# One block around the whole program, ordered by the scheduler's timing simulation (hybrid backbone, gated delta scan in chunks of 64)

## The chip, the core and the metric

The kernel runs on one core of a Trainium2 chip. The core has five engines, each with its own queue that it works through in order: TensorE (PE) for matmuls, VectorE (DVE), ScalarE (ACT), GpSimd (POOL), and SyncE (SP), which issues nearly all DMAs here. They meet through semaphores: an instruction waits at the head of its queue until what it needs is done, and everything behind it waits too. The metric is the device time of one execution in microseconds (us), lower is better; the numbers are medians over runs.

## What is computed

One inference step of a hybrid backbone with two layers, on 128 context tokens and 1024 latent tokens (nine tiles of 128 tokens in all), width 1024, in float32. The core of the reference:

```
def trunk_layer(x, cvec, lp, ctx):
    sh1, sc1, g1, sh2, sc2, g2 = jnp.split(jax.nn.silu(cvec) @ lp['w_ada'] + lp['b_ada'], 6, axis=-1)
    h = rmsnorm(x, lp['g_pre_mix']) * (1.0 + sc1) + sh1
    m, extras = mixing(h, lp, ctx)
    x = x + g1 * rmsnorm(m, lp['g_post_mix'])
    h = rmsnorm(x, lp['g_pre_ffn']) * (1.0 + sc2) + sh2
    f = conv_ffn(h, lp['w_up'], lp['ffn_conv_w'], lp['ffn_conv_b'], lp['w_down'])
    x = x + g2 * rmsnorm(f, lp['g_post_ffn'])
    return x, extras
```

`mixing` projects `h` once and splits the result among three groups: a conformer convolution (width 31, layer norm, swish); a gated delta net with four heads, scanned forwards and backwards in chunks of 64, whose step is

```
        v_new = ui - jnp.einsum('bhcd,bhde->bhce', wi, state)
        o = jnp.einsum('bhcd,bhde->bhce', qd, state) + jnp.einsum('bhij,bhje->bhie', it, v_new)
        state = state * gl[..., None, None] + jnp.einsum('bhcd,bhce->bhde', kd, v_new)
```

and neighbourhood attention with four heads. A second projection joins the three. The modulation (`w_ada`) is a vector product of its own.

## The kernel before, in words

The class `K` builds the program (L1639 and on, `run`), once for the whole network. Every large matmul is made in three passes with split operands: high by high, low by high, high by low (`mm3`, L429 to L431; the z gates and the attention's projections have the same three on L618). Such a group of 24 matmuls has 128x386 outputs and is called dense work here.

A layer runs in this order in the code:

- Start (layer 0 only): `ada_pe` loads the modulation weights (`rawa`, L315) and multiplies them (L317, L323); token tiles `x` come in on L406; `tail_weights` loads `rawt` (L494); each token tile is turned on PE (L387) and goes through the tail of the input projection.
- Heads 0 and 1 of the delta net: dense work (`gdn_dense`), decays, then `preps`, which inverts the chunk matrices: `fd` and `F` to and from memory (L677, L1619, L1629), `DA` loaded in eight pieces (L820), blocks multiplied on PE (L841, L854).
- `gdn_scan` of heads 0 and 1: 18 chunk steps forwards and backwards for each head. One step is L921 (state times keys and queries), `t` on DVE, L929, `ys` and `y` on ACT, L943 (state update) and L946, then two updates of `S` and an addition into `o` on DVE.
- While that scan runs, dense work of heads 2 and 3 (`gdn_piece`), of the convolution (`conf_dense`), its depthwise taps (`conf_conv`, the DVE operation named `cu`, in eight pieces of 31 taps, lowered in priority by `LOW`), and the inverse of heads 2 and 3 (operation `e` on DVE, L1626, L1627).
- Then the z gates, `gdn_out` of heads 0 and 1 (L993), the late part of heads 2 and 3 (`gdn_late`: loads `kq` L757, `DI` and `DA` L760, `ktm` L763, products L771, blocks), the attention's projections, and in layer 0 a part of the next modulation (`ada_fill`, L271 and L273).
- The scan of heads 2 and 3 with the attention woven into it. Its loads are `V` (L1217), `oq` from the cached keys (L1225), `qk` (L1233) and the bias `whib` and `RB` (L1168, in pieces); L1250 turns the cached keys.
- The convolution's output (`conf_out`, L1071 and L1102), more `ada_fill`, the output projection, and the feed-forward part with its own depthwise convolution.

What sets the order: the scheduler places the instructions of one block by its cost estimate and its priorities, and each engine's queue follows that placement. Three sections are exempt for PE, where the code says `manual_schedule(engines=ENG)` with `ENG = {PE}`: the start with the tail projection, the scan of heads 2 and 3 with the attention, and the end of a layer with the next one's tail. There PE's order is as written. SP, DVE, ACT and POOL have no section of that kind. The program was one block before and is one after.

Of the kernel before, what the change touches and what calls it, by code (L numbers as in the profile page):

```python
# [1783 lines left out]


def emit(tc, I, O):
    with ExitStack() as ctx:
        K(ctx, tc, I, O).run()


# [57 lines left out]
```

## Time and profile before

| | before |
|---|---|
| median of 3 runs | 3492.34 us |
| lowest, highest | 3491.82, 3495.67 us |
| the profiled execution, its own time | 3500.02 us |
| its span in the profile | 3498.2 us |
| mean granted clock of TensorE | 0.959 |
| PE busy | 3251.0 us (93%) |
| DVE busy | 2127.5 us (61%) |
| ACT, POOL busy | 1293.4 us (37%), 1026.5 us (29%) |

The profile shows each instruction with its start and duration; the span is first to last. The granted clock is 1 where TensorE has its 2.4 GHz and 0.5 where it has 1.2 GHz; a mean between them says what part of a stretch was at which. Stretches of one stage are compared by a table: length, then busy time of each engine with the instructions' number, then the clock. A wait is named after the instruction that waited and the one whose result came last.

### The profile page before, as it was taken

To read this page: it belongs to the slowest core of one execution; us is meant where nothing else is said; L and a number is where in the kernel's file an instruction comes from. 1 tells how busy PE (TensorE), PEld (TensorE's weight loads), DVE (VectorE), ACT (ScalarE), POOL (GpSimd) and SP (SyncE) were. 2 spreads that over 40 slices of the span, in tenths; PEclk is the share of its full clock that TensorE was granted. 3 is DMA by queue.
4 is the path that set the end of the run, shared out by engine and by line. 5 is a ranking of instruction groups with operands and counts; after the bars stand their busy time and mean duration, and the time that the engine had idled before them with its cause. 6 is when DMAs were issued, how large, how long until landed. Compare 5 with 4: busy or idle time off the path is not lost. (4 is left out here: it accounts for less than half of the span.)

```text
span 3498.2 us, 52694 instructions
## 1 busy us (share of the span) xinstructions
PE 3251.0 (93%) x19868; PEld 2842.8 (81%) x19868; DVE 2127.5 (61%) x4128; ACT 1293.4 (37%) x2887; POOL 1026.5 (29%) x933
## 2 busy tenths in 40 slices
PE   8999996978999999999989989879599999999997
PEld 5997775626899988989989977877388999999997
DVE  4677776744556666655476767878654444444446
ACT  4333333534433333333254423346443222222223
POOL 3421213123544334434234311221343112211114
PEclk9999998988999999999999999989699999999999
DMA  5332454255323222222134223642452111111113
GB/s 194 103 81 82 144 157 92 56 184 152 117 85 94 73 76 88 82 64 78 41 134 126 64 70 92 188 99 62 128 167 71 37 37 44 54 43 43 37 37 132
DMA packets 288339, 324.08 MB, mean 93 GB/s; under 512 B 152143, under 2 KB 213855, under 8 KB 286998
## 3 DMA queue, kind: packets, MB, share of 16 engines
q1 hardware_dynamic: 288086, 320.72, 30.8%
q8 instruction: 157, 2.57, 0.3%
q14 instruction: 96, 0.79, 0.1%
HBM read 250.68 MB, written 69.95 MB: 92 GB/s over the span
## 5 line engine op out<-in xcount | busy, mean ns | idle before, releaser
L431 PE MATMUL d<-hhi,wlo 128*128 128x386 f32 (+1 forms) x3072 | 1056.0, 344 | 5.5 <-POOL wlo L420 5.5
L429 PE MATMUL d<-hhi,whi 128*128 128x386 f32 (+1 forms) x3072 | 1056.3, 344 | 3.5 <-DVE cv L124 3.4
L430 PE MATMUL d<-hlo,whi 128*128 128x386 f32 (+1 forms) x3072 | 1055.4, 344 | 3.2 <-issue 3.2
L420 POOL TENSOR_TENSOR wlo<-raw,whi 128x1024 fp32r<-128x1024 f32 x136 | 343.6, 2527 | 1151.7 <-ACT whi L121 1082.9
L124 DVE SCALAR_TENSOR_TENSOR cv<-d,fvec,cv 128x384 f32<-128x384 f32 (+1 forms) x528 | 325.3, 617 | 459.5 <-ACT cv L121 451.0
L431 PEld LDWEIGHTS d<-hhi,wlo 128*128 128x128 f32 x3072 | 584.5, 190 | 18.5 <-issue 10.0
L429 PEld LDWEIGHTS d<-hhi,whi 128*128 128x128 f32 x3072 | 585.8, 191 | 14.6 <-issue 12.3
L430 PEld LDWEIGHTS d<-hlo,whi 128*128 128x128 f32 x3072 | 585.4, 191 | 7.4 <-issue 5.7
L1541 DVE TENSOR_TENSOR f<-d,f 128x512 f32<-128x512 f32 x360 | 245.2, 687 | 163.6 <-PE d L431 161.6
L121 ACT ACTIVATE cv<-d,fvec 128x384 f32<-128x384 f32 (+1 forms) x264 | 174.6, 663 | 440.9 <-PE d L431 432.4
L429 PE MATMUL d<-wdh,ahi 128*128 128x512 f32 x792 | 316.1, 399 | 11.0 <-DVE f L1541 9.1
L430 PE MATMUL d<-wdl,ahi 128*128 128x512 f32 x792 | 313.6, 396 | 0.0
L431 PE MATMUL d<-wdh,alo 128*128 128x512 f32 x792 | 312.7, 395 | 0.0
L124 DVE SCALAR_TENSOR_TENSOR cu<-cu,vec 128x292 f32<-128x292 f32 (+1 forms) x480 | 253.6, 554 | 4.0
L121 ACT ACTIVATE whi<-raw 128x1024 fp32r<-128x1024 f32 x136 | 143.6, 1056 | 161.4 <-PE d L430 132.1
L429 PEld LDWEIGHTS d<-wdh,ahi 128*128 128x128 f32 x792 | 149.1, 188 | 50.5 <-DVE f L1541 14.4
L223 POOL TENSOR_TENSOR adacc<-adacc,adpr 128x512 f32<-128x512 f32 x112 | 153.2, 1368 | 124.8 <-ACT adpr L121 97.1
L431 PEld LDWEIGHTS d<-wdh,alo 128*128 128x128 f32 x792 | 148.9, 188 | 36.1 <-issue 0.7
L430 PEld LDWEIGHTS d<-wdl,ahi 128*128 128x128 f32 x792 | 148.9, 188 | 34.3 <-issue 1.4
L121 ACT ACTIVATE adpr<-adraw,cs 128x512 f32<-128x512 f32 x112 | 80.9, 723 | 241.7 <-POOL adacc L223 193.0
L1528 POOL TENSOR_TENSOR wdl<-rawd,wdh 128x512 fp32r<-128x512 f32 x88 | 115.4, 1312 | 182.9 <-ACT wdh L121 182.9
L1517 DVE TENSOR_TENSOR alo<-sg,ahi 128x384 fp32r<-128x384 f32 x132 | 111.3, 843 | 70.8 <-ACT ahi L121 70.5
(349 smaller groups left out, 5222.4 us busy)
## 6 DMA issues: line engine op xcount, KB each, us to landing
raw<-in_w_up_t SPq DMA_DIRECT2D x88, 512.0 KB
adraw<-in_w_ada SPq DMA_DIRECT2D x112, 256.0 KB
raw<-in_w_in_t SPq DMA_DIRECT2D x48, 512.0 KB
rawd<-in_w_down SPq DMA_DIRECT2D x88, 256.0 KB
xs<-x SPq DMA_DIRECT2D x27, 512.0 KB
x<-xs SPq DMA_DIRECT2D x27, 512.0 KB
rawa<-in_w_ada SPq DMA_DIRECT2D x24, 512.0 KB
x<-in_x SPq DMA_DIRECT2D x18, 512.0 KB
```

The source lines that it names most:

```text
L121: return self.nc.scalar.activation(out=out, in_=in_, func=func, **kw)
L124: return self.nc.vector.scalar_tensor_tensor(out=out, in0=in0, scalar=s, in1=in1, op0=op0, op1=op1, **kw)
L223: nc.gpsimd.tensor_tensor(out=acc[:, 1, :], in0=acc[:, 1, :], in1=pr, op=ALU.add)
L420: nc.gpsimd.tensor_tensor(out=lo[:, :n], in0=raw[:, :n], in1=hi[:, :n].bitcast(F32), op=ALU.subtract)
L429: nc.tensor.matmul(out, shi, mhi, start=(i == 0), stop=False)
L430: nc.tensor.matmul(out, shi, mlo, start=False, stop=False)
L431: nc.tensor.matmul(out, slo, mhi, start=False, stop=(i == n - 1))
L1517: nc.vector.tensor_tensor(out=lo[:, :n], in0=sg[:, :n], in1=hi[:, :n].bitcast(F32), op=ALU.subtract)
L1528: nc.gpsimd.tensor_tensor(out=lo, in0=raw[:, :512], in1=hi[:].bitcast(F32), op=ALU.subtract)
L1541: nc.vector.tensor_tensor(out=f[t][:, cs], in0=ps, in1=f[t][:, cs], op=ALU.add)
```

## The change

`emit` puts the whole program into a block with `schedule_with_timeline_sim=True`, so that the scheduler takes its other, more detailed timing model for placing instructions. The instructions are the same on every engine (PE 19,868 with its waits left out, DVE 4,128); only their order, and with it the waits, differs.

```
 def emit(tc, I, O):
-    with ExitStack() as ctx:
-        K(ctx, tc, I, O).run()
+
+    with tc.block(schedule_with_timeline_sim=True):
+        with ExitStack() as ctx:
+            K(ctx, tc, I, O).run()
```

Line numbers above this place stay; the three manual sections keep PE's order. The first place that matters is the queue of SP at the start. Before:

```order
L315 DMA rawa<-in_w_ada 128x1024 x14
L494 DMA rawt<-in_w_tail 128x544
L315 DMA rawa<-in_w_ada 128x1024 x2
L494 DMA rawt<-in_w_tail 128x544 x2
L406 DMA x<-in_x 128x1024 x2
L494 DMA rawt<-in_w_tail 128x544
L406 DMA x<-in_x 128x1024 x5
L416 DMA raw<-in_w_in_t 128x1024 x2
L406 DMA x<-in_x 128x1024 x2
```

After, at the same place in the queue:

```order
L315 DMA rawa<-in_w_ada 128x1024 x6
L494 DMA rawt<-in_w_tail 128x544 x2
L406 DMA x<-in_x 128x1024 x4
L315 DMA rawa<-in_w_ada 128x1024 x4
L494 DMA rawt<-in_w_tail 128x544 x2
L315 DMA rawa<-in_w_ada 128x1024 x2
L406 DMA x<-in_x 128x1024 x3
L315 DMA rawa<-in_w_ada 128x1024 x2
L416 DMA raw<-in_w_in_t 128x1024 x2
L315 DMA rawa<-in_w_ada 128x1024 x2
L406 DMA x<-in_x 128x1024 x2
```

The modulation weights are spread among the token tiles, and their last two loads stand behind seven of these.

The second place is the scan of heads 0 and 1 in layer 0. DVE's queue in its middle, before (`t`, `S` and `o` are the scan's own; `cu` is the depthwise convolution, `cv` and `cp` the projections' short convolution):

```order
L124 SCALAR_TENSOR_TENSOR t<-a,ne,V 128x128
L124 SCALAR_TENSOR_TENSOR cu<-cu,vec 128x292 x2
L124 SCALAR_TENSOR_TENSOR t<-a,ne,V 128x128
L124 SCALAR_TENSOR_TENSOR cu<-cu,vec 128x292
L124 SCALAR_TENSOR_TENSOR S<-S,ex,b 128x128
L124 SCALAR_TENSOR_TENSOR S<-S,ex,c 128x128
```

After, also in the middle (`e` is the inversion of heads 2 and 3):

```order
L124 SCALAR_TENSOR_TENSOR S<-S,ex,b 128x128
L124 SCALAR_TENSOR_TENSOR S<-S,ex,c 128x128
L1626 TENSOR_TENSOR e<-e 72x368
L124 SCALAR_TENSOR_TENSOR cu<-cu,vec 128x291
L959 TENSOR_TENSOR o<-a,o 128x128
L124 SCALAR_TENSOR_TENSOR t<-a,ne,V 128x128
L124 SCALAR_TENSOR_TENSOR cu<-cu,vec 128x292
L1627 TENSOR_TENSOR e<-e 72x2x23x8
L124 SCALAR_TENSOR_TENSOR cu<-cu,vec 128x291
L124 SCALAR_TENSOR_TENSOR cu<-cu,vec 128x292
L1626 TENSOR_TENSOR e<-e 72x396
```

All eight pieces of `cu` and the whole inversion of heads 2 and 3 now stand inside this scan. PE's queue in the same scan's last steps, before:

```order
L929 MATMUL a<-V,XN 64x128 x2
L431 MATMUL d<-hhi,wlo 128x386
L921 MATMUL a<-S,kq 64x128 x3
L943 MATMUL b<-ys,ktm 128x128
L943 MATMUL c<-ys,ktm 128x128
L946 MATMUL a<-y,DI 64x128 x2
L921 MATMUL a<-S,kq 64x128
L429 MATMUL d<-hhi,whi 128x388
```

After:

```order
L929 MATMUL a<-V,XN 64x128 x2
L929 MATMUL a<-t,XN 64x128 x2
L943 MATMUL b<-ys,ktm 128x128
L943 MATMUL c<-ys,ktm 128x128
L946 MATMUL a<-y,DI 64x128 x4
L929 MATMUL a<-V,XN 64x128 x2
L921 MATMUL a<-S,kq 64x128 x4
```

No dense matmul is left between the last steps; all of it, the z gates' and the attention's projections too, stands ahead of them.

The third place is PE's queue behind the attention of layer 0, where the modulation fill (`b<-rawa,cs`) meets the convolution's output. Before:

```order
L273 MATMUL b<-rawa,cs 2x512 x8
L278 MATMUL b<-rawa,ones 2x512
L291 MATMUL b<-ident,rawa 128x2 x4
L1071 MATMUL a<-ident,cl 128x128 x4
L1102 MATMUL c<-ident,xh 128x128
L1071 MATMUL a<-ident,cl 128x128 x2
```

After:

```order
L993 MATMUL c<-ident,on 128x128 x18
L273 MATMUL b<-rawa,cs 2x512 x7
L1071 MATMUL a<-ident,cl 128x128 x2
L273 MATMUL b<-rawa,cs 2x512
L278 MATMUL b<-rawa,ones 2x512
L1071 MATMUL a<-ident,cl 128x128 x2
```

The convolution's transposes begin behind the first of four fill chunks, where before they followed the fourth; the output projection's matmuls follow among the later chunks. Besides this, SP's queue now has the attention's loads (`V`, `oq`, `qk`) ahead of the late heads' `kq`, `DI`, `ktm` and `DA`, where before it had them behind.

## Rows read from the trace of the kernel before

**Rows 1.** The page: busy time and share of each engine; the convolution's taps.

```profile
PE 3251.0 (93%) x19868; PEld 2842.8 (81%) x19868; DVE 2127.5 (61%) x4128; ACT 1293.4 (37%) x2887; POOL 1026.5 (29%) x933
...
L124 DVE SCALAR_TENSOR_TENSOR cu<-cu,vec 128x292 f32<-128x292 f32 (+1 forms) x480 | 253.6, 554 | 4.0
```

**Rows 2.** Stretches: length, busy us PE, PEld, DVE, ACT, POOL (count), clock, DMA share, GB/s.

```profile
0.00:86.10 86.10, 70.88 (x368) 51.68 (x369) 37.09 (x114) 39.17 (x73) 25.55 (x50) 0.96 0.58 197
...
278.10:391.90 113.80, 112.52 (x972) 77.67 (x971) 82.94 (x249) 46.92 (x165) 13.15 (x18) 1.00 0.22 66
391.90:567.50 175.60, 156.93 (x1120) 136.68 (x1118) 131.11 (x268) 56.02 (x161) 41.99 (x31) 0.94 0.53 156
567.50:741.40 173.90, 133.37 (x1222) 93.40 (x1222) 125.25 (x361) 87.27 (x277) 31.77 (x56) 0.85 0.35 74
741.40:784.10 42.70, 36.02 (x85) 6.29 (x83) 6.36 (x12) 10.66 (x20) 13.07 (x8) 0.90 0.85 284
784.10:813.50 29.40, 20.70 (x74) 14.35 (x74) 13.85 (x37) 10.96 (x22) 10.50 (x20) 0.65 0.34 100
...
935.00:1800.00 865.00, 854.36 (x4448) 791.14 (x4447) 522.61 (x738) 307.31 (x484) 336.17 (x234) 1.00 0.26 79
...
2060.00:2175.00 115.00, 110.82 (x946) 76.43 (x945) 80.68 (x242) 44.81 (x158) 10.33 (x7) 0.99 0.22 65
2175.00:2326.00 151.00, 140.72 (x1091) 133.13 (x1088) 125.71 (x257) 59.01 (x167) 38.48 (x40) 0.95 0.55 158
2326.00:2486.00 160.00, 129.61 (x1235) 94.00 (x1233) 130.39 (x372) 87.62 (x278) 32.15 (x56) 0.89 0.33 69
2486.00:2528.00 42.00, 14.68 (x41) 7.12 (x42) 23.20 (x52) 18.04 (x37) 21.42 (x27) 0.50 0.55 171
...
2650.00:3498.00 848.00, 828.85 (x4310) 774.68 (x4309) 414.83 (x612) 234.33 (x370) 187.15 (x114) 0.99 0.15 52
```

**Rows 3.** Waits of PE: waiter, cause, us in all, times, longest; whole span.

```profile
PE P L1250 <- DMA oq<-in_cache: 23.5, 2, 11.8
...
PE a L929 <- DVE t L124: 10.5, 7, 5.7
PE a L841 <- DVE XN L832: 10.4, 2, 5.6
...
PE a L921 <- DVE o L959: 6.1, 1, 6.1
```

**Rows 4.** The first 90 us: GB/s in 40 slices; the ada matmuls; PE's timeline (start, us).

```profile
GB/s 47 95 54 324 377 413 393 297 300 317 282 280 325 282 351 346 363 364 262 237 240 304 317 226 212 1 58 0 68 1 58 0 3 55 58 7 58 174 20 143
...
L317 PE MATMUL d<-rawa,cb x64: 592/592/1190, 9.1 to 39.2; 128*128 128x512 f32 x64
...
46.91 0.59 PE L429 MATMUL d<-thi,hhi 128*128 128x272 f32 x1 [0.47 <-ACT hhi L121]
```

**Rows 5.** Timeline of the first step of the scan of heads 0, 1.

```profile
278.13 0.66 PE L921 MATMUL a<-S,kq 128*64 128x128 f32 x8
...
281.51 0.34 DVE L124 SCALAR_TENSOR_TENSOR S<-S,ex,c 128x128 f32<-128x128 f32 x1
```

**Rows 6.** Stretches of `cu` alone (DVE, clock); one of all engines as in 2.

```profile
660.00:742.00 82.00, 31.41 (x62) 0.80 0.24 65
2420.00:2490.00 70.00, 28.86 (x56) 0.86 0.22 55
...
580.00:600.00 20.00, 6.92 (x54) 5.16 (x52) 4.32 (x14) 3.64 (x10) 1.52 (x4) 0.66 0.76 106
```

**Rows 7.** Issues of the `DA` pieces (ns min/median/max, first to last start); layer 1's next scan.

```profile
L820 SPq DMA_DIRECT2D DA<-fy x32: 326/496/2552, 253.1 to 2277.1; - x32
...
2329.39 0.66 PE L921 MATMUL a<-S,kq 128*64 128x128 f32 x8
```

## The prediction

> **What bounds the kernel now.** I read the page's busy times first. TensorE (PE) is busy 93% of the span and VectorE (DVE) 61% [rows 1], so a new order can win only what PE loses: its idle time and its time at the lower clock level. Then I read a table of stretches [rows 2]; the reader is to compare PE's busy time with the stretch's length, and the granted clock with 1. Both feed-forward stages (865 and 848 us) keep PE busy 854 and 829 us at a clock of 0.99 or more: nothing to win in half of the span. The losses lie in the mixing stages: start (70.9 of 86.1), scan of heads 2 and 3 with the attention (133.4 of 173.9 at 0.85 in layer 0, 129.6 of 160 at 0.89 in layer 1), the modulation fill and the convolution's output in layer 0 (56.7 of 72.1), the latter in layer 1 (14.7 of 42 at 0.50). Third, the waits of PE [rows 3]: the largest is L1250, which waits twice some 11.8 us for the DMA that brings the cached keys `oq`.
>
> **What the change moves.** No instruction is added or removed. The sum is made on the profiled execution (3500.0 us, 3498.2 of them span) and carried to the median, which is 7.7 us lower, by difference.
>
> *Feed-forward.* Both orders agree here but for a place or so: 0.
>
> *Start: loss.* SP issues its loads in turn. Before, all 16 `rawa` loads stand ahead of the token tiles, with one `rawt` among them; after, the last two stand behind 7 token tiles of 512 KB, 3 more `rawt` of 272 KB and 2 `raw` of 512 KB, 5.4 MB. The slices of the DMA row show about 330 GB/s while the loads run [rows 4], so these land 16 us later. The last ada matmul starts at 39.2, the first tail matmul at 46.9 [rows 4]. The modulation vector gates every token's turn, so about 16 us pass through, less some 5 us since the tokens then are already there and the first transposes done (the 7.7 us from 39.2 to 46.9 shrink). +11, bounds 0 (PE was itself the slower: 64 matmuls took from 9.1 to 39.2) and +16.
>
> *Preparation of heads 0 and 1: gain.* L841 waits 4.8 and 5.6 us, once per layer [rows 3]. After, some 15 us more of dense matmuls stand ahead of it. That dense work is only brought forward, so just the wait goes: -8 for both layers, bounds -10 and 0.
>
> *Scan of heads 0 and 1 and the late preparation of heads 2 and 3.* Here is the heart of it. Before, PE's scan instructions have 2 to 8 dense matmuls between them, and the rest of the dense work covers the late chain. In layer 0 the stretch from scan to scan is 113.8 + 175.6 = 289.4 us with 112.5 + 156.9 = 269.4 us of PE work; in layer 1 115 + 151 = 266 with 251.5 [rows 2]. After, 14 to 30 dense matmuls stand between a step's instructions until the dense work is used up. Adding the trace's durations of what now stands from the first to the last scan instruction: PE 240 us, of the 269.4 in layer 0; 15 went ahead of the scan and 14 stand behind it. DVE gets the convolution's `cu` (218 in place of 40, at some 0.5 us in a row [rows 1]) and the inversion's `e`: 83.0 becomes 216 us. So PE stays the longer engine, but with less margin. I reckon 10 us of idle for that. The last 11 of 36 steps have under 4 us of PE work each: two heads run in alternation, and a step alone takes from 278.13 to 281.85, 3.7 us [rows 5]. Six such pairs need 25 us; PE's work of 19 us is inside. Filled part 222 + 10 + 25 = 257. Then the late chain, bare: loads, blocks, inverse, with 14 us of PE work. For heads 0 and 1 it took from the first `DA` load at 253.1 to the first scan matmul at 278.1, 25 us [rows 5, 7], beside dense work; the steps ahead of that (`kq` products, `DA` and `DI`) and the output transposes add about 10. I take 35; bounds 20 and 60. Layer 0: 15 + 257 + 35 = 307 against 289.4: +18. Layer 1, by the same way: 13 + 241 + 35 = 289 against 269 up to its next scan: +20. Bounds for each -10 and +45. What covers the late chain today is the dense work of the z gates and attention projections; that cover is what the change spends.
>
> A rule of the Trainium skill speaks against this move: "Perfetto Trace Analysis", section "Optimization Strategy", says that where the contended engine changes over time, interleaving those regimes can help. Before, a chain-bound regime and a PE-bound one are interleaved for the late heads, and the trace agrees in so far as PE is busy 157 of 175.6 us there; after, they are apart. How much that costs is the first rival below.
>
> *Attention with the scan of heads 2 and 3: gain.* PE's order is written by hand in this section and stays. SP issues the loads of the attention (`V`, `oq`, `qk`) after the change ahead of the late heads' own `kq` loads, where before they follow them and the late chain. So the 11.7 us at L1250 should go, in each layer. DVE no longer has the convolution here: 31.4 us of `cu` in 660 to 742, 28.9 in layer 1 from 2420 on [rows 6], and the L929 and L921 waits of 5.7 and 6.1 us [rows 3] are waits for DVE results queued behind it. -23.5 in layer 0. With fewer holes PE should be less at the lower level: 580 to 600 runs at 0.66 with 6.9 us busy [rows 6]; I add -6. -29, bounds -50 (idle 40.5 and some clock) and -10. Layer 1 has only the 11.8 and some 4 us of L929: -18, bounds -35 and -5.
>
> *Convolution output, modulation fill, output projection: gain.* In layer 0 PE did four chunks of fill, then the convolution's transposes, then the projection. After, transposes begin behind the first chunk, and projection triples fill between chunks. Idle there is 72.1 - 56.7 = 15.4 us, and the clock is 0.90 and 0.65 [rows 2], which by the stretch lengths is 4 + 10 us of clock. Idle and half of the rest, less what the fill's own loads still hold back (DMA share 0.85): -17, bounds -30 and 0. In layer 1 only a few triples move ahead of the last transposes: -4, bounds -15 and +5.
>
> **Sum.** 11 - 8 + 18 + 20 - 29 - 18 - 17 - 4 = -27. 3492.3 - 27 = 3465.
>
> **Rivals.**
> - *Slower: the bare late chain.* Its place is between the last scan step of heads 0, 1 and the first of heads 2, 3. For: in layer 1 it took 52 us from its last `DA` load at 2277.1 to the scan at 2329.4 [rows 7], and nothing fills it now. Against: the chain then shared PE and DVE with other work. At 60 us per layer in place of 35, with the loads waiting for buffers that the scan frees last, the sum is -27 + 50 = +23: 3515. It decides from 35 + 13.5 = 48 us per layer on.
> - *Slower: the waits of the attention stay.* Earlier in SP's queue helps only where the buffer is free and the data are there. If both waits and the holes remain, 29 + 18 come back: +20, 3512. Against: `oq` is filled from an input, in a queue that had late loads ahead of it.
> - *The order changes little.* PE is in order and 93% busy; gains in the attention and costs in the scan could cancel within 7 us: 3492.
> - *More gain.* The late chain begins in the last scan steps, since its `kq` products stand among them in PE's new order. Then the +18 and +20 fall to about 0: -65, 3427.
>
> **How the numbers follow.** Forecast (-8 to -55) 0.46, more gain 0.12, little change 0.13, bare chain 0.19, waits stay 0.10. Hence faster by over 0.2% (about what a measurement of this kernel can tell from no change, 7 us) 0.58, within 0.13, slower 0.29. The range for 8 in 10 runs from 3425 (more gain) to 3525 (bare chain, with a late start); as forecasts of both signs hold much of the chance, the likeliest one's own range is 3437 to 3484.
>
> **What would show it.** Right: the wait of L1250 is gone from PE's waits; no `cu` during the attention; attention stretches of some 145 us; the first tail matmul near 58 us; a hole of some 20 to 25 us of PE idle between the two scans. The scan of heads 0 and 1 should last about 257 us in layer 0 with PE busy over 0.9 of it until its last steps. Wrong: a late stretch over 48 us, DVE the engine that PE waits for all along the scan (then 216 us of DVE work was not the smaller load), or L1250 still waiting.

## The result and the profile after

The new order is slower: 3537.43 us median (3532.86 to 3538.2) against 3493.8 us for the kernel before on the same chip, a ratio of 1.0122 with a 95% interval of [1.0105, 1.014]. The forecast was 3465, faster; the range of 3425 to 3525 does not hold the time either. The profiled execution has a span of 3535.6 us, 37.4 more than before, at a mean granted clock of 0.947 in place of 0.959.

The page of the new order, its busy times and the taps:

```profile
PE 3268.9 (92%) x19868; PEld 2857.9 (81%) x19868; DVE 2159.0 (61%) x4128; ACT 1295.5 (37%) x2887; POOL 1037.3 (29%) x933
...
L124 DVE SCALAR_TENSOR_TENSOR cu<-cu,vec 128x292 f32<-128x292 f32 (+1 forms) x480 | 252.8, 557 | 0.9
```

Against [rows 1] the instructions are the same in number, and the taps cost the same. PE is busy 17.9 us more with the same matmuls: they ran longer, at the lower clock level.

The table of stretches of the new order (length, then busy us of PE, PEld, DVE, ACT, POOL with counts, clock, DMA share, GB/s). In layer 0: start; scan of heads 0 and 1; from scan to scan; attention; convolution output and fill; projection; FFN. In layer 1: from scan to scan; attention; convolution output; projection:

```profile
0.00:90.10 90.10, 71.46 (x369) 51.51 (x370) 39.74 (x114) 39.04 (x73) 25.89 (x50) 0.96 0.50 190
294.30:549.90 255.60, 242.13 (x1627) 192.65 (x1627) 217.12 (x527) 75.91 (x215) 46.40 (x49) 0.97 0.41 119
549.90:606.20 56.30, 29.95 (x398) 21.43 (x397) 24.98 (x48) 30.64 (x113) 17.41 (x22) 0.50 0.58 147
606.20:755.00 148.80, 128.55 (x1216) 92.37 (x1216) 90.27 (x280) 83.19 (x272) 16.54 (x32) 0.89 0.21 52
755.00:825.70 70.70, 64.50 (x192) 23.59 (x192) 21.93 (x48) 20.27 (x40) 23.09 (x28) 0.86 0.67 222
825.70:956.20 130.50, 111.88 (x532) 94.83 (x532) 60.84 (x100) 56.79 (x121) 57.01 (x72) 0.95 0.44 140
956.20:1791.90 835.70, 825.45 (x4312) 768.08 (x4313) 511.16 (x712) 297.61 (x466) 328.06 (x219) 0.99 0.25 76
2314.10:2367.40 53.30, 28.87 (x395) 20.63 (x396) 24.82 (x47) 31.49 (x115) 16.18 (x19) 0.53 0.62 163
2367.40:2514.20 146.80, 128.21 (x1217) 92.41 (x1218) 90.25 (x279) 83.18 (x272) 16.48 (x32) 0.90 0.21 48
2514.20:2561.60 47.40, 29.27 (x104) 20.37 (x103) 21.47 (x45) 18.33 (x36) 23.17 (x28) 0.63 0.47 156
2561.60:2693.00 131.40, 113.15 (x534) 95.40 (x532) 62.64 (x99) 56.98 (x119) 56.02 (x71) 0.94 0.43 139
```

Read it beside [rows 2]. The scan has swallowed the dense work (255.6 us, PE busy 0.95 of it), and what follows it is naked, that is, the late chain runs there with no dense work beside it: 56.3 us with 29.95 of PE work at a clock of 0.50, and 53.3 us in layer 1. The attention is the gain, 148.8 in place of 173.9 us.

PE's longest waits in the new order (us in all, times, longest):

```profile
PE c L993 <- DVE zt L124: 38.2, 14, 8.6
PE d L429 <- DVE cv L124: 25.8, 4, 8.1
PE d L429 <- ACT chi L121: 16.5, 3, 8.3
...
PE a L929 <- DVE t L124: 9.7, 10, 3.2
```

The same three first waits in the kernel before:

```profile
PE c L993 <- DVE zt L124: 19.4, 7, 4.8
...
PE d L429 <- ACT chi L121: 5.5, 3, 4.2
...
PE d L429 <- DVE cv L124: 5.1, 5, 1.8
```

L1250, the largest of [rows 3], is gone as forecast, and the longest at L929 is 3.2 in place of 5.7 us. What grew in their place is L993 (the output of the heads; 22.9 of its 38.2 us lie in the two naked stretches), L429 for `chi` (the projection), and L429 for `cv`, of which 16.0 us are the FFN's first taps of the two layers.

The account by stages, from the two traces with the same marks (end of the start, first instruction of each scan, last transposed output of the attention, first tap of the FFN; the FFN of layer 0 ends with its last `cv` on ACT). The last column is what the term was off by:

| stage | forecast | measured | off |
|---|---|---|---|
| start | +11 | 90.0 - 86.1 = +3.9 | -7 |
| to the scan of heads 2, 3, layer 0 | -4 + 18 = +14 | 516.3 - 481.5 = +34.8 | +21 |
| attention, layer 0 | -29 | 148.8 - 173.9 = -25.1 | +4 |
| convolution output, projection, layer 0 | -17 | 201.2 - 198.0 = +3.2 | +20 |
| FFN, layer 0 | 0 | 835.8 - 839.2 = -3.4 | -3 |
| to the scan of heads 2, 3, layer 1 | -4 + 20 = +16 | 575.5 - 550.8 = +24.7 | +9 |
| attention, layer 1 | -18 | 146.8 - 160.8 = -14.0 | +4 |
| convolution output, projection, layer 1 | -4 | 178.8 - 164.7 = +14.1 | +18 |
| FFN and end | 0 | 842.5 - 843.4 = -0.9 | -1 |
| sum | -27 | +37.3 | +64 |

Two groups of terms make nearly all of it: the way to the second scan (+29) and the stretch from the attention to the FFN (+38). The experiments go to these two, and to the attention, where the forecast came out but its reasons had not been taken apart. One caution holds for all of them: an edit gives the scheduler a new program, and other places move by a few us too. In the four kernels below whose edit leaves the stretch from the attention to the FFN alone (the bias pieces, the other buffer, the two with cover), it took 195.8 to 201.6 us in layer 0 and 177.2 to 180.1 in layer 1. So a stage's length is compared first, the total second, and a few us in a stage are little.

### The profile page after: what moved, and what is told of

Read it like the earlier page. It is cut to its first block, busy times and chain, and to the rows that moved or that the text cites. A ratio compares the mean times of both kernels' runs of the same rounds, so it can differ in the third digit from the quotient of the medians.

```text
span 3535.6 us, 52748 instructions
## 1 busy us (share of the span) xinstructions
PE 3268.9 (92%) x19868; PEld 2857.9 (81%) x19868; DVE 2159.0 (61%) x4128; ACT 1295.5 (37%) x2887; POOL 1037.3 (29%) x933
## 5 line engine op out<-in xcount | busy, mean ns | idle before, releaser
L429 PE MATMUL d<-hhi,whi 128*128 128x386 f32 (+1 forms) x3072 | 1052.9, 343 | 26.7 <-DVE cv L124 25.8
L429 PEld LDWEIGHTS d<-hhi,whi 128*128 128x128 f32 x3072 | 584.0, 190 | 36.0 <-ACT cv L121 16.6
L429 PE MATMUL d<-wdh,ahi 128*128 128x512 f32 x792 | 317.3, 401 | 8.4 <-DVE f L1541 8.4
L429 PEld LDWEIGHTS d<-wdh,ahi 128*128 128x128 f32 x792 | 149.4, 189 | 46.8 <-DVE f L1541 12.7
L1528 POOL TENSOR_TENSOR wdl<-rawd,wdh 128x512 fp32r<-128x512 f32 x88 | 116.1, 1319 | 171.3 <-ACT wdh L121 171.2
```

The lines of the kernel that those rows point to most:

```text
L429: nc.tensor.matmul(out, shi, mhi, start=(i == 0), stop=False)
L1528: nc.gpsimd.tensor_tensor(out=lo, in0=raw[:, :512], in1=hi[:].bitcast(F32), op=ALU.subtract)
```

## Experiments on the naked late chain

**Bias pieces in SP's queue.** In the new order, loads of the attention's bias (`whib`, `RB`) stand on SP among the late heads' loads. This kernel puts the bias pieces (L1168) behind the last `DA` load, which it keeps in `lastDA` (what stands under `issue_after(x)` comes behind x in its queue):

```
+            with self.tc.issue_after(self.lastDA):
                 nc.sync.dma_start(out=RB[...], in_=I["rpb"][...])
```

> The new order, with one edit: the 64 small loads of the attention's bias (RB, whib) of a layer are issued by SP behind the last DA load of the late heads, not between the loads of the late chain. Theory (SP's queue sets the length of the late chain, some 85 issues in 41 us at 0.48 us each, about half of them bias): the stretch between the two scans falls from 56 and 53 us to about 42 each, and part is given back where the attention waits for its bias; in all 3505 to 3525 us. Rival (the chain of blocks, inverse and copies sets it, whoever issues): both stretches stay above 50 us and the time within 6 us of 3537.

Measured: 3531.32 us, ratio 1.0118 [1.0094, 1.0141]; the naked stretches 52.8 and 55.5 us where they were 56.3 and 53.3. The pieces were not what held it.

**Another buffer for `DA`.** `gdn_late` puts `DA` into the buffer with the tag `o`, in which the output of the first scan's head lies until `gdn_out` has read it. SP's queue in the new order, from 555.86 us (start, us, instruction):

```profile
555.86 4.12 SPq L1168 DMA_DIRECT2D whib<-in_rpb  x7
560.08 0.94 SPq L1004 DMA_DIRECT2D cat<-zt  x2
561.07 0.78 SPq L1168 DMA_DIRECT2D whib<-in_rpb  x2
561.94 0.35 SPq L760 DMA_DIRECT2D DA<-dec  x1
```

The first `DA` load of the late heads goes out at 561.94, 12 us after the scan's end at 549.9, and the loads of the blocks (L820) only from 566.46 on. This kernel lets `DA` and the scan's `V` change places:

```
-        DA = hpool.tile([...], F32, tag="o", name="DA", bufs=1)
+        DA = hpool.tile([...], F32, tag="V", name="DA", bufs=1)
-        V = hpool.tile([...], F32, tag="V", name="V", bufs=1)
+        V = hpool.tile([...], F32, tag=vtag, name="V", bufs=1)
```

(`vtag` is "o" for the late heads, and their output takes "V".)

> The new order, with the late heads' DA tile put into the place of the values V of heads 0 and 1, which the scan frees, in place of the tile of their outputs o, which gdn_out frees last; the late V takes the place of o. Theory (in the bare late chain DA waits for gdn_out of the same place, at 562 and 576 us in the profile, so the two chains run one behind the other): the stretch between the scans falls from 56 and 53 us to 40 to 45 each, the time to 3505 to 3518 us. Rival (the chain is as long without that wait): both stretches above 50 us, time within 6 us of 3537.

SP's queue after the edit, from the scan's end at 550.0:

```profile
550.26 0.42 SPq L760 DMA_DIRECT2D DI<-dec  x1
550.73 0.36 SPq L1168 DMA_DIRECT2D RB<-in_rpb  x1
551.14 5.78 SPq L820 DMA_DIRECT2D DA<-fy  x4
```

The stretch of layer 0 in that kernel, columns as above:

```profile
550.00:595.60 45.60, 26.74 (x396) 20.88 (x395) 19.31 (x43) 24.68 (x98) 11.10 (x18) 0.54 0.61 158
```

Measured: 3523.61 us, 1.0088 [1.0063, 1.0112], 14 us under the new order's median, though the two intervals still touch; the naked stretches 45.6 and 45.1 us. `DA`'s blocks now load 15 us earlier, and 8 to 11 us of each naked stretch were this buffer. First scan and chain together took 301.3 us in layer 0 and 281.4 in layer 1; the new order and the four kernels that leave both alone (stores, order of the code, low parts, FFN's vector) lie at 311.9 to 316.6 and 290.3 to 299.6. The remaining 45 us are still 10 above the 35 forecast.

**Why 45 and not 35.** The same instructions stand in the trace before, beside dense work. The groups of PE in its stretch from 391.9 to 567.5 (busy us, mean ns, idle before):

```profile
L993 PE MATMUL c<-ident,on 128*128 128x128 f32 x18 | 4.5, 288 | 4.6 <-DVE zt L124 3.4 <-ACT on L121 1.2
L841 PE MATMUL a<-XN,DA 32*32 32x32 f32 x144 | 3.6, 192 | 0.0
...
L655 PE MATMUL a<-ident,kq 128*128 128x128 f32 x18 | 2.8, 282 | 0.0
```

and in the naked stretch of the new order, 549.9 to 606.2:

```profile
L993 PE MATMUL c<-ident,on 128*128 128x128 f32 x18 | 7.0, 454 | 12.4 <-DVE zt L124 11.9 <-ACT on L121 0.6
L841 PE MATMUL a<-XN,DA 32*32 32x32 f32 x144 | 6.1, 238 | 2.9 <-DVE XN L832 1.9 <-DVE XN L828 0.9
L655 PE MATMUL a<-ident,kq 128*128 128x128 f32 x18 | 5.1, 433 | 5.5 <-ACT XN L121 2.9 <-ACT junk L121 2.2 <-DVE XN L812 0.3
```

A transpose takes 454 ns in place of 288. With the dense work gone, PE falls to its 1.2 GHz level (0.50), and the chain's own matmuls run slower. The idle part, 56.3 - 29.95 = 26.4 us, is close to the 20 to 25 that the forecast gave; the PE work inside it is 30 us where the forecast had put 14. Not all of that is the clock. 14 us fit the blocks and the `kq` products and transposes of the trace before (L841, L854, L856, L771, L655 for `kq`: 3.6, 2.5, 2.4, 3.1, 2.8); bare, with 52 of the 72 products in the stretch, they are busy 6.1, 3.9, 3.9, 3.6 and 5.1. The transposes of the outputs and of `vT`, 8.6 us before and 12.4 bare, stood in the forecast's "about 10". (The groups overlap a little, so they add up to more than 30.)

**Cover given back, first try.** The attention's projections, which the new order runs inside the first scan, are queued behind that scan's last matmul:

```
+            with self.tc.issue_after(self.ends[mybir.EngineType.PE]):
+                for i in range(2):
+                    self.attn_dense(l, i, hh, gc)
```

> The new order, with the attention's projections (and by it the z gates of heads 2 and 3 behind them) queued on PE behind the last matmul of the scan of heads 0 and 1, so that dense work is left for the late chain. Theory (the loss is the cover that was spent): scan from 256 to about 185 us, the stretch to the next scan from 56 to 85 to 100 us with PE busy over 0.85 of it, net -25 to -35 us a layer, 3470 to 3490 us. Rival (the scan's steps run bare instead, so the loss only moves): scan above 215 us or PE idle over 40 us in it, time above 3520 us.

Stretches of this kernel in layer 0: from scan to scan, attention, and the scan of heads 0 and 1:

```profile
505.30:590.80 85.50, 85.22 (x727) 67.89 (x725) 20.10 (x46) 35.36 (x120) 14.30 (x10) 0.98 0.54 164
590.80:768.90 178.10, 152.29 (x1357) 116.61 (x1356) 98.83 (x289) 94.25 (x293) 36.54 (x62) 0.91 0.35 80
294.60:505.30 210.70, 172.88 (x1159) 130.94 (x1158) 201.58 (x519) 60.06 (x185) 27.21 (x32) 0.73 0.30 86
```

Measured: 3569.74 us, 1.0225 [1.0202, 1.0248], worse than the new order. The late chain is covered (PE busy 85.22 of 85.50), but the scan is now the naked one: DVE is busy 201.58 of its 210.7 us, with taps and the inversion in it, while PE has 172.88 us of work and drops to a clock of 0.73. So I took the taps in the scan for a second cost of the same order, one that makes DVE the bound as soon as PE's cover goes elsewhere. The next kernel tests it.

**Cover given back, second try.** As before, and five of the eight pieces of taps are queued on DVE behind the scan's last DVE instruction:

```
-            with self.tc.high_priority(-LOW):
+            with self.tc.high_priority(-LOW), self.tc.issue_after(self.ends[mybir.EngineType.DVE]):
                 self.conf_conv(l, range(NCV, 8), pcp)
```

> The new order, with the attention's projections queued on PE behind the scan of heads 0 and 1 as in the run with cover, and five of eight pieces of the convolution's taps queued on DVE behind that scan too. Theory (in the run with cover the scan was held by DVE, 202 of 211 us busy, since all taps stood in it): scan 150 to 175 us, stretch to the next scan 75 to 90, attention 165 to 180, that is near the kernel before in each, time 3490 to 3515 us. Rival (bare steps, not the taps, hold the scan): scan above 195 us, time above 3545 us.

From scan to scan, attention and first scan of layer 0:

```profile
458.60:574.60 116.00, 112.25 (x865) 94.04 (x863) 101.80 (x208) 43.80 (x137) 27.38 (x16) 0.97 0.53 157
574.60:729.70 155.10, 127.18 (x1217) 91.81 (x1216) 93.44 (x282) 85.81 (x276) 30.75 (x56) 0.89 0.35 70
294.70:458.60 163.90, 147.10 (x1159) 114.13 (x1158) 137.55 (x363) 58.46 (x184) 26.87 (x32) 0.92 0.35 105
```

Measured: 3492.63 us, 0.9996 [0.9982, 1.001]. Scan and late chain together take 279.9 us (264.8 in layer 1), where the new order has 311.9 (292.8) and the kernel before 289.4 (265.9). With cover and taps spread again the loss of 1.2% is gone. What came back here, 32 and 28 us, is more than that loss: the attention gave up 6.3 and 12.0 us of its gain (L1250 waits again, 9.8 and 5.2 us), and the stretch to the FFN stayed as long as in the new order (201.0 and 180.1 us). This is the strongest result on the cause: where the dense work and the taps stand against the scan and the chain is worth some 60 us. The taps held without the cover were not run, so the two parts' shares are open.

## Experiments on the stretch from the attention to the FFN

**Stores on another queue.** In layer 1, SP's last two stores of the convolution's output take 5.44 us from 2557.64 on, since the second waits for its data, and the projection's loads of `oc` stand behind them. (In the kernel before the same two take 7.74.) This kernel issues these stores from GpSimd's queue:

```
-                    nc.sync.dma_start(out=self.cat[c][...], in_=yh[:, :w])
+                    nc.gpsimd.dma_start(out=self.cat[c][...], in_=yh[:, :w])
```

> The new order, with the convolution's output stored (cat<-yh) from GpSimd's queue in place of SP's. Theory (SP stands at these stores, with the first loads of the attention's output for the projection queued behind): PE's waits of 8.3 and 7.8 us for chi fall below 3 us each, time 3520 to 3530 us. Rival (PE's own late transposes of the convolution set the start of the projection, or GpSimd's issues cost as much): waits move elsewhere and the time stays within 5 us of 3537, or rises.

Measured: 3544.72 us, 1.0154 [1.0131, 1.0178]; the waits for `chi` 9.0 and 9.4 us where they were 8.3 and 7.8. Refuted. SP reaches the load of `oc` early now and still stands until the convolution's last step. I read that as a matter of memory (`oc` lies in a pool opened after the convolution's is closed); no run here separates it.

**PE in the order of the code.** The new order mixes projection matmuls into the convolution's transposes on PE. Here that section's PE order is written order:

```
+                with self.tc.manual_schedule(engines=ENG):
                     for x in (ads, co, ws):
                         run(x)
                     ...
                     self.out_proj(l, W, hh2, pool)
```

> The new order, but PE's order from the modulation fill over the convolution's output to the end of the output projection is the code's, as it nearly was before: fill, then all transposes of the convolution, then the projection. Theory (interleaving the projection with the convolution's output costs the 14 us that the stretch from the end of attention to the feed-forward part grew by in layer 1): that stretch goes from 179 to 163 to 168 us in layer 1 and stays at 196 to 202 in layer 0; time 3520 to 3527 us. Rival (the late end of the attention and the other queues' order set it): 175 us or more in layer 1, time 3533 us or more.

Measured: 3562.33 us, 1.0191 [1.0168, 1.0213]; the stretch to the FFN 216.4 and 177.3 us, against 201.2 and 178.8. Undoing the mixing gives nothing back in layer 1 and costs 15 us in layer 0, so on balance the mixing is not the loss.

**The weights' low parts held back.** In the new order the 16 subtractions `rlo` that split the output weights stand between the convolution's own small steps on GpSimd and DVE. GpSimd's timeline in layer 1:

```profile
2526.25 3.29 POOL L1420 TENSOR_TENSOR rlo<-rraw,rhi 128x512 fp32r<-128x512 f32 x2
2529.63 0.69 POOL L132 TENSOR_SCALAR brs<-bmv 128x1 f32<-128x1 f32 x1
2530.40 1.33 POOL L1420 TENSOR_TENSOR rlo<-rraw,rhi 128x512 fp32r<-128x512 f32 x1
2531.82 0.69 POOL L132 TENSOR_SCALAR brs<-bmv 128x1 f32<-128x1 f32 x1
2532.59 0.54 POOL L135 TENSOR_TENSOR brs<-brs,mh 128x1 f32<-128x1 f32 x1
2533.09 1.28 POOL L1420 TENSOR_TENSOR rlo<-rraw,rhi 128x512 fp32r<-128x512 f32 x1
```

`brs`, one number per token, waits behind blocks of 1.3 us and more; from the first `brs` to the last pass 23.9 us (2516.2 to 2540.2), against 18.5 before (2490.7 to 2509.2). The edit queues each `rlo` behind the fourth pair's statistics, and moves the whole splitting (`ws`, all but its first loads) behind the convolution's output in the code:

```
+                with self.tc.issue_after(self.gate[n]):
                     e.tensor_tensor(out=lo[:, c], in0=raw[:, c], in1=hi[:, c].bitcast(F32), op=ALU.subtract)
...
-                    if i >= WS:
-                        next(ws, None)
+                    if i == WS:
+                        next(ws)
```

> The changed kernel, with the output weights' low parts (the 16 subtractions `rlo` on VectorE and GpSimd) held back on both queues until the conformer branch's fourth pair of tiles has its statistics. If the conformer's last stage is slow because these subtractions stand between its steps, it takes about 33 us in layer 1 in place of 47, the stretch from the attention's end to the FFN's first tap falls from 178.8 to about 166 us, and the time to about 3523. If what holds it is the order of TensorE, or SyncE's, the stretch stays at 177 to 181 us and the time within 5 us of 3537.

Stretch from attention to FFN, layers 0 and 1:

```profile
752.70:948.00 195.30, 174.99 (x724) 116.72 (x724) 86.67 (x148) 76.69 (x160) 79.11 (x100) 0.95 0.53 174
...
2499.20:2670.50 171.30, 139.66 (x636) 113.81 (x635) 85.15 (x144) 74.82 (x155) 79.43 (x99) 0.87 0.46 150
```

Measured: 3529.04 us, 1.0103 [1.0077, 1.0129], not separable from the new order's 1.0122 in the total. In the stage, 5.9 and 7.5 us less, and the longest wait for `chi` 3.3 us in place of 8.3. Both figures are upper ones: the profiled execution took 3515.55 us, 13.5 less than the median, and its attention, which the edit leaves alone, is 3.3 and 4.1 us shorter too. In layer 0, 195.3 us is hardly less than the 195.8 of a kernel without the edit; in layer 1, 171.3 lies clear of 177.2. So it is a part of the cause in layer 1, at most 7.5 of the 12.8 expected, by the trace of the stage.

Nor is it `brs` alone: its chain in layer 1 shortened only to 21.9 us (2501.2 to 2523.1), and its last pass still stands behind `rlo`. More came behind it. In the new order 63 projection matmuls stand on PE between the last `xh` and its last transpose, which starts 19.9 us later; in this kernel it is 21 matmuls and 13.6 us, before the change none and 6.3 us.

**The FFN's vector.** The load `fvec` of the FFN's taps goes out at 2690.8 in the new order, and PE stands 8.08 us at the first tap. Its tile lies in memory that the projection frees last. Here it gets a place that is free earlier:

```
-        self.fvec = epool.tile([128, 176], F32, name="fvec", bufs=1)
+                self.fvec = hp2.tile([128, 176], F32, name="fvec", bufs=1)
```

(with the load moved ahead of the projection; `hp2` holds the FFN's input)

> The changed kernel, with the FFN's vector of taps and biases in the pool of the FFN's input, so that its load doesn't wait for the projection's pool to come free. If the two holes of 7.9 and 8.1 us on TensorE at the FFN's start come from that load, they go, and the time falls by 14 to 16 us, to about 3522. If another wait stands right behind it, the holes stay above 5 us, and the time is 3532 to 3538.

PE's timeline at the first tap of layer 1 in this kernel, and below it a wait that grew:

```profile
2706.88 0.66 PE L429 MATMUL d<-hhi,whi 128*128 128x388 f32 x1 [5.89 <-DVE cv L124]
...
PE a L771 <- DMA kq<-gs: 13.9, 2, 8.2
```

Measured: 3547.75 us, 1.0162 [1.0141, 1.0183]. The holes fell from 7.9 and 8.1 to 5.9 us each, and no further: the first tap then waits for the last token tile itself, whose split (`hlo` on GpSimd, then `cv` on ACT) is the next one late. So the load is worth 2 us of each hole. In the kernel before, `fvec` goes out just as late (2652.71, the first `cv` at 2654.8), and PE has other work there and no hole. The stretch gained 2.5 and 3.7 us; elsewhere the new placement lost more, for one at L771 (13.9 us in place of 7.6). A miss.

## Experiments on the attention's gain

**Cached keys loaded early, in the kernel before.** One part of the change alone: `oq` in a tile of its own, loaded with the first bias tiles.

```
+        self.koq = pool.tile([128, H, 64], F32, name="koq", bufs=1)
+        nc.sync.dma_start(out=self.koq, in_=I["cache"][l, 0].rearrange("h s d -> s h d"))
-            nc.sync.dma_start(out=kraw[:, :, i, :], in_=I["cache"][l, 0].rearrange("h s d -> s h d"))
+            nc.gpsimd.tensor_copy(out=kraw[:, :, i, :], in_=self.koq)
```

> The kernel before, in its old order, with the cached keys loaded once, early, into a tile of their own and copied by GpSimd into the place where the transposes read them. Theory (the wait of L1250 for this load, 11.7 us a layer, is a loss by itself, so taking it early gives it back as the new order did): 3472 to 3482 us. Rival (the attention's other operands are late too, so another wait takes its place): L1250's wait goes, the time stays within 6 us of 3493.

Measured: 3486.86 us, 0.9979 [0.9963, 0.9995], a gain of 0.2%. The wait of 11.7 us at L1250 went, but attention fell by 4.6 and 2.0 us only: in layer 0, `vctx`, loaded from the same cache, waits 4.5 us in its place, and L929 grew from 6.2 to 9.3.

**Taps early, first try.** `NCV = 8` in the kernel before, so that all eight pieces stand early in the code.

> The kernel before, in its old order, with all eight pieces of the convolution's taps emitted in the scan of heads 0 and 1, where three were. Theory (the new order's gain in the attention comes from DVE being free of taps there): attention from 174 and 161 us to 155 to 162 and 146 to 152, time 3465 to 3478 us, if the late stage has room for them. Rival (the gain came from the loads): attention within 5 us of before, time 3488 to 3500 us.

Measured: 3490.42 us, 0.9989 [0.9972, 1.0005]. The low priority that these pieces carry kept them where they were (31.42 us of `cu` in 660 to 742, as in [rows 6]), so this tested nothing.

**Taps at ordinary priority, in the kernel before.** `LOW = 3000` becomes `LOW = 0`.

> The kernel before, with the conformer's taps at ordinary priority: by the program's order all 496 then stand ahead of the second scan, where 74 and 70 of them stood beside the attention. This is one part of the change alone. If these taps are what the attention of the kernel before waits for, attention falls from 174 and 161 to about 150 and 147 us while the late stage grows by no more than 10 us: 3460 to 3475. If not, attention stays above 168 and 157 and the time within 8 us of 3493, or above it where the late stage grows by what attention loses.

PE's timeline in this kernel, the longest new wait of each layer (start, length, in brackets the wait):

```profile
498.31 0.69 PE L431 MATMUL d<-hhi,wlo 128*128 128x386 f32 x1 [13.50 <-POOL wlo L420]
...
2361.37 0.69 PE L929 MATMUL a<-t,XN 64*64 64x128 f32 x4 [17.85 <-DVE t L124]
```

Measured: 3529.92 us, 1.0111 [1.0089, 1.0133], a loss. In layer 0 attention did fall, from 173.9 to 160.6, with 0.8 us of taps left in it and L1250 still waiting 9.0 (11.7 before, so 2.7 of the 13.3 are not the taps'). But the late stage grew from 175.2 to 198.1, with the 13.50 us for `wlo` in it (last section). In layer 1 it grew from 150.2 to 159.1, and DVE still had 22.7 us of taps to work off when the second scan began: the scan's first `t` stood 17.85 us behind them, and the attention grew from 160.8 to 176.0. So taps in the attention do cost there (some 11 us in layer 0), and moved in a block they cost as much or more elsewhere.

**All of it together.** The second cover kernel with the `rlo` hold, the early `fvec` and the early cached keys; no other edit.

> The changed kernel with its cover given back (projections of the attention and five conformer pieces queued behind the scan, 3492.6 before), and with the output weights' low parts held, the FFN's vector loaded early and the cached keys loaded early. If the terms add, 3492.6 - 16 (FFN's start) - 12 (conformer's end) - 12 (waits of 9.8 and 5.2 for the cached keys, less 3) gives about 3453, faster than both kernels by over 1%. If each wait that goes only uncovers the next one, 3480 to 3492.

The waits of PE that are left:

```profile
PE d L429 <- DVE cv L124: 20.7, 4, 5.9
PE c L993 <- DVE zt L124: 18.1, 10, 3.4
PE c L1104 <- ACT yh L121: 14.3, 9, 5.0
```

Measured: 3483.46 us against 3490.84, 0.9969 [0.9951, 0.9986]: faster than both kernels, by 0.3% over the one before. The terms did not add up to 3453. Against the second cover kernel the stretch to the FFN gave 11.2 us in layer 1, which bears out the holds there, and lost 2.9 in layer 0, the attention gave 1.1 and 4.3 us, and each wait that went had another close behind it.

## Why the prediction was wrong

*What held.* The scan of heads 0 and 1: 257 and 241 us forecast, 255.6 and 239.5 measured, with PE busy 242.13 where 240 had been added up. The attention: 25.1 and 14.0 us won against 29 and 18, no `cu` in it, no wait at L1250. The reasons are half settled: in layer 0 the idle time of PE fell from 40.5 to 20.2 us, 11.7 of it at L1250; the two parts done alone gave 4.6 and 13.3 us of the 25.1. The FFN: unchanged. The start came out milder, the first tail matmul at 51.7 where 58 was forecast, +3.9 and not +11.

*The late chain, +40 us.* Here the step "Then the late chain, bare ... I take 35" failed; the two layers have 56.3 and 53.3. The forecast's own first rival set its turning point at 48 us, and this is that rival. The direction of the term was right, its size was not, and two things made it so. The PE work inside was priced at the durations of a trace in which dense matmuls ran beside it at a clock of 0.94; bare, at 0.50, a transpose takes 454 ns in place of 288, and the groups that the 14 us fit are busy 22.6. And `DA` shares a buffer with the first heads' output, so that its loads wait for `gdn_out`; the swap gave 8 to 11 us back. The rival as written ("with the loads waiting for buffers that the scan frees last") named that place, with a chance of 0.19. In layer 1 some 11 us came back at another place: the stretch from the FFN to the first scan took 282.6 us where it had taken 284.9, though 13 us of dense work had been counted into it. And two readings were loose: the 269 us of layer 1 are 265.9 from scan to scan, and six pairs of 3.7 us are 22, not 25. So the two stages are off by 29 and not by 40.

The rule that I set beside this move (the Trainium skill, "Perfetto Trace Analysis", section "Optimization Strategy", on interleaving regimes whose bounds differ) bears out in these runs: a chain-bound stretch and a PE-bound one laid apart cost 311.9 us in layer 0, woven together again, with five pieces of taps held back too, 279.9.

*Convolution output and projection, +38 us.* The step "transposes begin behind the first chunk, and projection triples fill between chunks" failed: forecast -17 and -4 us, measured +3.2 and +14.1. It looked at PE's queue alone, and at its start. In layer 0 the convolution's output does begin sooner, its first transpose of `xh` 14.9 us behind the attention's end in place of 45.7, but it ends as far behind it as before (72.1 us, before 72.6), and SP's loads of `oc` for the projection go out only then (at 828.8). The projection triples that fill PE stand ahead of its last transposes, and the splitting of the output weights, in queues of DVE and GpSimd that I did not read, between its small steps. With the splitting held, layer 1 gave at most 7.5 us back. The FFN's first tap then waits 8 us per layer, where the trace before has no such hole; 2 us of each are the load of `fvec`. In layer 0 that ate the gain; in layer 1, where there was little to gain, it is a plain loss. What was given back by these edits is at most half of the 38 us; the rest is open.

*The sum.* Start, first scans, attention and FFN came within 7 us each. The bare chain missed by 21 and 18 us, and the stretch from attention to FFN by 20 and 18: one was priced at a clock and with buffers that it did not have, the other by one engine's queue out of five.

## What to carry to other kernels

When an order moves cover away from a dependency chain, price the chain as it will run then: its TensorE work at the lower clock level, and its loads from the moment that their buffers come free. Read every queue of the stretch, not only the busiest engine's, and to the end of the chain in it: here small steps on GpSimd with larger ones put among them took 23.9 us in place of 18.5, and work that filled PE held the chain's last transposes back. And a gain from one wait removed should be counted only up to the next wait behind it: 11.7 us here became 4.6.

## What the hardware showed that I had not expected

A GpSimd subtraction can be held for many times its length by an unbroken row of DVE work. In the kernel with the taps at ordinary priority, `wlo` (128x1024, median 2.404 us) took 17 us twice among 136 times, once in each layer. The row gives min, median and max in ns:

```profile
L420 POOL TENSOR_TENSOR wlo<-raw,whi x136: 2337/2404/17085, 87.1 to 3456.9; 128x1024 fp32r<-128x1024 f32 x136
```

The one of layer 0 stood from 481.20 to 498.26 beside 38 DVE instructions, all of them `cu` and `e` in turn, without a gap of 0.05 us; PE stood 13.50 us for it. The one of layer 1, the longest, stood beside 38 such instructions too. At the end DVE is the one held. DVE's timeline at the end of the one in layer 0:

```profile
495.79 0.27 DVE L1626 TENSOR_TENSOR e<-e 72x116 f32<-72x116 f32 x1
495.98 2.60 DVE L124 SCALAR_TENSOR_TENSOR cu<-cu,vec 128x292 f32<-128x292 f32 x1
498.50 2.44 DVE L1627 TENSOR_TENSOR e<-e 72x116 f32<-72x116 f32 x1
500.87 0.51 DVE L124 SCALAR_TENSOR_TENSOR cu<-cu,vec 128x292 f32<-128x292 f32 x1
```

A `cu` of 0.51 us took 2.60, to about the time that `wlo` ended, and an `e` of 0.27 us took 2.44 beside the next `wlo`, which began there and took 2.587. The Trainium skill, "SBUF — State Buffer", section "SBUF: two separate sides", says that VectorE operations with two SBUF inputs and GpSimd operations that read SBUF share a port pair, and that whichever starts first has it for the whole instruction while the other is blocked. The trace agrees, both ways round, and shows besides that GpSimd can lose to a whole row of DVE instructions, over 14 us here (481.20 to 495.98), not only to one. The longest `wlo` in the kernel before took 8.820 us and ended 2.2 us after a row of 14 `cu` without a gap. A price of GpSimd work next to an unbroken row on DVE, read from the median, would have been some 15 us too low here.
